# Chaining the four column-group matmuls of each modulation step, with one weight tile per step

## The chip, the core and the metric

The kernel runs on one core of a Trainium2 chip. The metric is device microseconds (us) of one execution, median of three runs. The core has TensorE (PE; its weight loads are shown apart as PEld), VectorE (DVE), ScalarE (ACT), GpSimd (POOL) and SyncE (SP). In this kernel SP issues the transfers from device memory. Each engine takes its instructions in the order of the program, and semaphores tie the engines together.

## The reference, cut to what matters

Two blocks run one after the other on a sequence of 256 tokens, width 1024, all in f32. The first has a hybrid layer (attention with a window, beside a gated delta rule) and a recurrent layer, each followed by an MLP. The second has two layers whose streams (the sequence, and a context of 256 tokens) are scaled and shifted by six vectors of 1024 that come from two conditioning vectors alone:

```python
def modulation(cvec, w_mod, b_mod):
    m = jax.nn.silu(cvec) @ w_mod + b_mod        # w_mod: 1024 x 6144 for each layer
    return jnp.split(m[:, None, :], N_MOD, axis=-1)

    for i in range(DEPTH):                        # second block
        ml = modulation(c, w_mod[i], b_mod[i])
        mc = modulation(c_ctx[None, :], w_mod[i], b_mod[i])
        hl = modulate(rmsnorm(xl, g_pre_mix[i]), ml[0], ml[1])
        ...
```

Nothing in the first block depends on the modulation, so its matmuls can stand anywhere before the second block's layers need them.

## The kernel before, in words

**Main work.** Every large weight matrix is cut into units of 1 MB (tile `wr`, two buffers). ACT rounds each half of a unit to a reduced f32 type (`wh`, line 407), DVE subtracts to get the rest (`wl`, line 408), and PE multiplies `wh` and `wl` with the activations, which are split the same way; results collect in the PSUM tiles `pa`, `pb` and `pc`. Four halves may be held at a time (`NW = 4`). All matmuls go through the helper `mm` (line 342) and all transposes through `tr` (line 366), so that these two lines stand for most of PE's work. Matmuls of the delta rule and of the attention are on plain f32 operands; each f32 matmul leaves two records in the trace.

**Delta rule.** `level` (line 1006 and after) builds a triangular inverse up in six levels for each of two halves of the sequence: POOL makes a masked copy (line 1009), PE multiplies it, ACT copies the product (line 1013), PE multiplies twice more, DVE subtracts (lines 1020 and 1021). After it `delta_out` walks through the two chunks, product by product.

**Modulation.** `mods` (line 749 and after) is a generator of 48 steps: 2 layers x 3 thirds of the 6144 columns x 8 blocks of 128 rows. In one step the two conditioning vectors (`cs_t`, padded to 32 columns) are the stationary operand, and 128 rows x 2048 columns of the weights stream past it as four matmuls of 512 columns. Each of the four writes other 32 partitions of one PSUM bank (`pm`), so each uses another group of 32 columns of the PE array. Eight steps add up into one `pm`; then DVE takes it out (line 782), and some of it goes through device memory (`mdr`).

**Weights of the modulation.** A step's 1 MB comes as two tiles of 512 KB (`wm`, four buffers), loaded by SP in `mod_load` (line 737), two steps ahead. SP's one queue holds these loads and those of `wr` in program order; a load whose buffer is not free holds up what stands behind it.

**Order.** The code calls `fill(n)` at chosen places and weaves the generator between other generators. Then a scheduler orders every engine's instructions by a priority, which is the place in the code unless `tc.high_priority` moves it, and by its own estimate of when an instruction could start. The four matmuls of a step stand in `high_priority(-10)`: ten places later than written.

Of the kernel before, what the change touches and what calls it, by code (L numbers as in the profile page):

```python
# [10 lines left out]
F32 = mybir.dt.float32  # L11
# [4 lines left out]
P = 128  # L16
BIG = 1.0e30
SM = 1.0 / math.sqrt(96.0)
NW = 4
LEAD = 96  # L20
TRAIL = 24
# [9 lines left out]
def _unit(w, k0, nk, cols):  # L31

    n = w.shape[1]
    a = w.reshape(-1, P, n)[k0 : k0 + nk][:, :, cols]
    return a.transpose(1, 0, 2).reshape(P, -1)
# [83 lines left out]
def _ncols(c):  # L119
    return c.stop - c.start if isinstance(c, slice) else len(c)  # L120
# [62 lines left out]
def _consts():  # L183

    parts, at = ([], []), [0, 0]

    def add(name, a, hyb=0):
        a = np.asarray(a, np.float32).reshape(P, -1)
        KC[name] = (hyb, at[hyb], a.shape[1])
        at[hyb] += a.shape[1]  # L190
        parts[hyb].append(a)

    i = np.arange(P)[:, None]
    j = np.arange(P)[None, :]
    add("ident", np.eye(P))
    add("tri", i <= j, 1)
    add("mask_s", np.where(j >= i, BIG, 0.0), 1)
    add("mask_t", np.where(j < i, -BIG, 0.0), 1)
    for s in (1, 2, 4, 8, 16, 32, 64):
        add(f"lv{s}", (i // (2 * s) == j // (2 * s)) & (i % (2 * s) >= s) & (j % (2 * s) < s), 1)  # L200
    add("amask", np.concatenate([np.where(j > i, 0.0, -BIG), np.where(j <= i, 0.0, -BIG)], 1), 1)
    half = 32
    inv = np.float32(10000.0) ** (-np.arange(half, dtype=np.float32) / np.float32(half))
    ang = (np.arange(256, dtype=np.float32)[:, None] * inv[None, :]).astype(np.float32)
    c, s = np.cos(ang.astype(np.float64)), np.sin(ang.astype(np.float64))
    add("cos", np.concatenate([c, c], 1).reshape(2, P, 64).transpose(1, 0, 2), 1)
    add("sin", np.concatenate([-s, s], 1).reshape(2, P, 64).transpose(1, 0, 2), 1)
    inv = (1.0 / (np.float32(10000.0) ** (np.arange(0, 16, 2, dtype=np.float32) / np.float32(16)))).astype(np.float32)
    row = np.repeat(np.arange(4), 64).astype(np.float32)
    col = np.tile(np.arange(64), 4).astype(np.float32)  # L210
    ar, ac = row[:, None] * inv, col[:, None] * inv
    ang = np.concatenate([ar, ar, ac, ac], 1).astype(np.float64)
    c, s = np.cos(ang), np.sin(ang)
    sg = np.where(np.arange(32) % 16 < 8, -1.0, 1.0)
    s = s * sg
    add("acos", c.reshape(2, P, 32).transpose(1, 0, 2))
    add("asin", s.reshape(2, P, 32).transpose(1, 0, 2))
    ft = np.zeros((P, 256))
    ft[64:96] = c.T
    ft[96:128] = s.T  # L220
    ft *= -SM
    add("aft", ft)
    lo = np.arange(P) < 64
    add("one", np.stack([~lo, 0 * lo, lo], 1))
    return [np.ascontiguousarray(np.concatenate(p, axis=1)) for p in parts]


def _pack(inputs):
    def t(name):
        return np.asarray(inputs[name])  # L230

    units = _weight_units(t)
    sizes = [(nk * _ncols(c), nk) for _, _, nk, c in units]
    wp = np.zeros((len(units), P, 2048), np.float32)
    for n, un in enumerate(units):
        a = _unit(*un)
        wp[n, :, : a.shape[1]] = a
    wm = np.ascontiguousarray(
        t("w_mod_2").reshape(2, 8, P, 3, 2, 1024).transpose(0, 3, 1, 4, 2, 5)
    )  # L240
    one = np.ones(1024, np.float32)
    bg = []
    for i in range(2):
        b = t("b_mod_2")[i].reshape(12, 512)
        g = np.concatenate(
            [one, t("g_pre_mix_2")[i], t("g_post_mix_2")[i], one, t("g_pre_mlp_2")[i], t("g_post_mlp_2")[i]]
        ).reshape(12, 512)
        bg.append(np.stack([b, g], 1).reshape(3, 4, 1024))
    cc = np.zeros((P, 8, 32), np.float32)
    cc[:, :, 0] = t("c_2")[0].reshape(8, P).T  # L250
    cc[:, :, 1] = t("c_ctx_2").reshape(8, P).T
    x = t("x")[0]
    kc0, kc1 = _consts()
    arrays = {
        "x": np.ascontiguousarray(x.reshape(2, P, 1024)),
        "xT": np.ascontiguousarray(x.T.reshape(8, P, 256).transpose(1, 0, 2)),
        "ctx": np.ascontiguousarray(t("ctx_2")[0].reshape(2, P, 1024)),
        "wp": wp,
        "wm": wm,
        "bg": np.ascontiguousarray(np.stack(bg)),  # L260
        "cc": cc,
        "cols": np.ascontiguousarray(_cols(t)),
        "rows": _rows(t),
        "kc": kc0,
        "kch": kc1,
    }
    return arrays, sizes
# [26 lines left out]
def hybrid_then_mla(ctx: ExitStack, tc: tile.TileContext, a, out, usizes):  # L294
    nc = tc.nc
    V, S, G, T = nc.vector, nc.scalar, nc.gpsimd, nc.tensor
    cpool = ctx.enter_context(tc.tile_pool(name="cpool", bufs=1))
    wpool = ctx.enter_context(tc.tile_pool(name="wpool", bufs=1))
# [8 lines left out]
    def nm(s):  # L307
        uid[0] += 1
        return f"{s}_{uid[0]}"
# [22 lines left out]
    def psC():  # L332
        return psp.tile([P, 512], F32, tag="pc", bufs=1, name=nm("pc"))

    def psM():
        return psp.tile([P, 512], F32, tag="pm", bufs=1, name=nm("pm"))
# [2 lines left out]
        return ap.bitcast(F32)  # L339

    def mm(o, l, r, start, stop):
        T.matmul(o, l, r, start=start, stop=stop)  # L342

    def v3(ap, n):
        return ap.rearrange("p (a b) -> p a b", a=n)
# [19 lines left out]
    def tr(o, i):  # L365
        T.transpose(o, i, ident)  # L366


    class WS:
        raw, hl, nd, nsp, ng, vec, ahead = {}, {}, 0, 0, 0, set(), 0  # L370
# [24 lines left out]
    def w_split():  # L395
# [5 lines left out]
        r = WS.raw[u][:, o : o + n]  # L401
        h = wpool.tile([P, 1024], F32R, tag="wh", bufs=NW, name=f"wh{i}")
        l = wpool.tile([P, 1024], F32R, tag="wl", bufs=NW, name=f"wl{i}")
        if u in WS.vec:
# [310 lines left out]
    cs_t = cpool.tile([P, 8, 32], F32, name="cs_t")  # L715
# [9 lines left out]
    class WM:  # L725
        tiles, n = {}, 0

    def mod_load():

        if WM.n >= 48:  # L730
            return
        i, q, k = WM.n // 24, WM.n // 8 % 3, WM.n % 8
        for j in range(2):
            wm = wpool.tile([P, 2, 512], F32, tag="wm", bufs=4, name=nm("wm"))
            if WM.n < 2:
                G.tensor_copy(wm[:, 0, 0:1], WM.after)
            nc.sync.dma_start(out=wm, in_=a["wm"][i, q, k, j].rearrange("p (a b) -> p a b", a=2))
            WM.tiles[WM.n, j] = wm
        WM.n += 1

    mc = cpool.tile([P, 2, 3, 32], F32, name="mc")
# [7 lines left out]
    def mods():  # L749

        def cols_of(m, i, q):
            pt = psC()
            for c in range(4):
                tr(pt[:, 128 * c : 128 * c + 128], m[:, 128 * c : 128 * c + 128])
            V.tensor_copy(mc[:, i, q].rearrange("p (c r s) -> p c r s", c=4, r=4),
                          pt.rearrange("p (c r s) -> p c r s", c=4, r=4)[:, :, :, 0:2])

        todo = None
        for n in range(48):
            i, q, k = n // 24, n // 8 % 3, n % 8  # L760
            if k == 0:
                ps = psM()
            if k == 1 and todo:
                cols_of(*todo)
            if k == 4:
                bg = s4([P, 2, 512])
                for r in range(4):
                    nc.sync.dma_start(
                        out=bg[32 * r : 32 * r + 32],
                        in_=a["bg"][i, q, r : r + 1].rearrange("o (a b) -> o a b", a=2).to_broadcast([32, 2, 512]),  # L770
                    )
            while WM.n < min(n + 2, 48):
                mod_load()
            for r in range(4):
                with tc.high_priority(-10):
                    mm(ps[32 * r : 32 * r + 32, :], cs_t[:, k, :], WM.tiles[n, r // 2][:, r % 2, :], k == 0, k == 7)
            mod_load()
            if k < 7:
                yield
                continue  # L780
            m = s2([P, 512])
            V.tensor_tensor(m, ps, bg[:, 0, :], op=ADD)
            V.scalar_tensor_tensor(m, m, K("one")[:, q : q + 1], bg[:, 1, :], op0=ADD, op1=MUL)
            for r in range(4):
                if 2 * q + r // 2 in (2, 5):
                    nc.sync.dma_start(
                        out=mdr[i, :, 2 * q + r // 2, 512 * (r % 2) : 512 * (r % 2) + 512], in_=m[32 * r : 32 * r + 2]
                    )
            todo = (m, i, q)
            yield  # L790
        cols_of(*todo)
        yield
# [796 lines left out]
    def queries(m, s, wq):  # L1589
# [4 lines left out]
        for h2 in range(4):  # L1594
# [7 lines left out]
            if s == 0:  # L1602
                S.activation(qs, p3[0:96], AF.Identity, scale=-SM)
            else:
                S.activation(qs[0:64], p3[0:64], AF.Identity, scale=-SM)
                t1 = s2([P, 2, 256])
# [460 lines left out]
```

## Time and profile before

| | us |
|---|---|
| median of 3 runs | 1634.34 (1633.84 to 1636.41) |
| profiled execution, whole | 1635.88 |
| its span in the trace | 1633.8 |
| PE busy | 1578.0 (97%) |
| DVE busy | 1029.0 (63%) |
| ACT busy | 743.3 (45%) |
| mean granted TensorE clock | 0.991 of full |

Busy time is the time in which at least one instruction of an engine is under way; matmuls overlap in the pipeline, so what a matmul costs is read from start to start of its neighbours, not from its duration. The chain of work that ended last is followed from the last instruction back, at each step to what released it; its shares say on what the end of the program depended.

### The profile page before, as it was taken

To read this page: it belongs to the slowest core of one execution; us is meant where nothing else is said; L and a number is where in the kernel's file an instruction comes from. 1 tells how busy PE (TensorE), PEld (TensorE's weight loads), DVE (VectorE), ACT (ScalarE), POOL (GpSimd) and SP (SyncE) were. 2 spreads that over 40 slices of the span, in tenths; PEclk is the share of its full clock that TensorE was granted. 3 is DMA by queue.
4 is the path that set the end of the run, shared out by engine and by line. 5 is a ranking of instruction groups with operands and counts; after the bars stand their busy time and mean duration, and the time that the engine had idled before them with its cause. 6 is when DMAs were issued, how large, how long until landed. Compare 5 with 4: busy or idle time off the path is not lost.

```text
span 1633.8 us, 24905 instructions
## 1 busy us (share of the span) xinstructions
PE 1578.0 (97%) x10182; PEld 1358.9 (83%) x10182; DVE 1029.0 (63%) x1593; ACT 743.3 (45%) x1264; POOL 94.8 (6%) x121
## 2 busy tenths in 40 slices
PE   7999999999999999999999999999999999989998
PEld 7866679888878998877877789999999788779997
DVE  6874575556787556768974753444444789775555
ACT  5642244443574445436454543222222475554443
POOL 0021000000000000003010100000000030000000
PEclk9999999999999999999999999999999999989999
DMA  7865475555665554562310432222232262235553
GB/s 289 288 217 172 167 258 196 204 207 191 248 258 181 194 192 169 181 227 80 130 52 27 138 134 89 93 103 85 97 104 79 100 216 107 73 126 201 181 186 124
DMA packets 46946, 259.77 MB, mean 159 GB/s; under 512 B 5600, under 2 KB 5856, under 8 KB 24304
## 3 DMA queue, kind: packets, MB, share of 16 engines
q1 hardware_dynamic: 46832, 258.18, 44.9%
q8 instruction: 80, 1.31, 0.3%
q14 instruction: 34, 0.28, 0.1%
HBM read 257.08 MB, written 1.08 MB: 158 GB/s over the span
## 4 chain that ended last, share of the span: by engine, by line
PE 78%; DVE 8%; ACT 4%; DMA 2%; POOL 1%; issue 1%; POOLq 0%; DVEq 0%; ACTq 0%; SPq 0%
PE pa L342 44%; PE pb L342 27%; PE pm L342 4%; PE pb L366 2%; DVE wl L408 1%; DMA wr<-in_wp_dram 1%; PE pc L366 1%; ACT s L1389 1%; ACT wh L407 1%; DVE s L1583 1%; POOL ti L1395 1%; ACT s L1652 0%; DVE s L645 0%; DVE b L711 0%; DVE xt L1426 0%
## 5 line engine op out<-in xcount | busy, mean ns | idle before, releaser
L408 DVE TENSOR_TENSOR wl<-wr,wh 128x1024 fp32r<-128x1024 f32 (+2 forms) x366 | 443.4, 1217 | 301.4 <-ACT wh L407 288.4
L407 ACT CAST wh<-wr 128x1024 fp32r<-128x1024 f32 (+2 forms) x364 | 376.1, 1041 | 405.8 <-PE pa L342 202.6
L342 PE MATMUL pa<-wh,b 128*128 128x512 f32 (+3 forms) x1456 | 411.1, 365 | 12.5 <-ACT b L816 5.7
L342 PE MATMUL pb<-b,wh 128*128 128x256 f32 x2240 | 406.2, 284 | 0.0
L342 PEld LDWEIGHTS pb<-b,wh 128*128 128x128 f32 x2240 | 352.7, 192 | 7.2 <-issue 3.4
L342 PE MATMUL pb<-b,wl 128*128 128x256 f32 x1120 | 317.8, 284 | 0.0
L342 PEld LDWEIGHTS pa<-wh,b 128*128 128x128 f32 x1456 | 267.6, 195 | 57.1 <-ACT b L648 6.1
L342 PE MATMUL pa<-wl,b 128*128 128x512 f32 (+3 forms) x728 | 258.7, 364 | 8.9 <-DVE wl L408 8.9
L342 PE MATMUL pa<-wh,s 128*128 128x512 f32 x768 | 244.5, 391 | 0.0
L342 PEld LDWEIGHTS pb<-b,wl 128*128 128x128 f32 x1120 | 215.1, 192 | 1.7 <-issue 1.7
L342 PE MATMUL pa<-b,wh 128*128 128x256 f32 x1056 | 199.2, 289 | 3.7 <-ACT wh L407 1.9
L342 PEld LDWEIGHTS pa<-b,wh 128*128 128x128 f32 x1056 | 166.2, 193 | 16.0 <-issue 4.4
L342 PEld LDWEIGHTS pa<-wl,b 128*128 128x128 f32 x728 | 142.3, 195 | 35.3 <-DVE wl L408 13.5
L342 PEld LDWEIGHTS pa<-wh,s 128*128 128x128 f32 x768 | 144.4, 188 | 28.9
L342 PE MATMUL pa<-b,wl 128*128 128x256 f32 x528 | 150.1, 288 | 1.3 <-DVE wl L408 1.3
L342 PE MATMUL pa<-wl,s 128*128 128x512 f32 x384 | 150.4, 392 | 0.0
L342 PEld LDWEIGHTS pa<-b,wl 128*128 128x128 f32 x528 | 101.6, 193 | 8.2 <-DVE wl L408 3.3
L560 DVE TENSOR_TENSOR s<-s 128x512 f32<-128x512 f32 x80 | 54.9, 687 | 50.2 <-ACT s L558 50.2
L342 PE MATMUL pm<-wm,cs_t 128*32 128x512 f32 x384 | 83.2, 606 | 1.9 <-DMA wm<-in_wm_dram 1.7
L342 PEld LDWEIGHTS pa<-wl,s 128*128 128x128 f32 x384 | 72.3, 188 | 14.5 <-DVE wl L408 1.2
L1583 DVE SCALAR_TENSOR_TENSOR s<-cu,cols_sb,s 128x512 f32<-128x512 f32 (+1 forms) x120 | 70.7, 621 | 0.5
L366 PE MATMUL pb<-kc_sb,s 128*128 128x128 f32 x366 | 56.8, 279 | 10.8 <-DVE s L1408 2.5
(278 smaller groups left out, 1391.6 us busy)
## 6 DMA issues: line engine op xcount, KB each, us to landing
wr<-in_wp_dram SPq DMA_DIRECT2D x176, 1024.0 KB, 4.8
wm<-in_wm_dram SPq DMA_DIRECT2D x96, 512.0 KB, 5.2
row<-in_rows_dram SPq DMA_DIRECT2D x10, 512.0 KB, 5.5
wr<-in_wp_dram SPq DMA_DIRECT2D x4, 832.0 KB
s<-in_bg_dram SPq DMA_DIRECT2D x24, 128.0 KB, 5.6
row<-mdr SPq DMA_DIRECT2D x6, 512.0 KB, 3.5
wr<-in_wp_dram SPq DMA_DIRECT2D x4, 264.0 KB, 3.6
b<-in_xT_dram SPq DMA_DIRECT2D x4, 256.0 KB, 6.1
```

The costliest lines, as they stand in the source:

```text
L342: T.matmul(o, l, r, start=start, stop=stop)
L366: T.transpose(o, i, ident)
L407: S.copy(h[:, :n], r)
L408: V.tensor_tensor(l[:, :n], r, f(h[:, :n]), op=SUB)
L560: V.tensor_tensor(q, r, r, op=MUL)
L1389: S.activation(j, x, AF.Square, scale=scale, accum_out=o)
L1395: G.tensor_tensor(r, e, half[:, :1], op=POW)
L1583: V.scalar_tensor_tensor(ac, src, w(k), ac, op0=MUL, op1=ADD)
```

## The change

The weights of one step become one tile of 1 MB, and three such tiles are held, loaded three steps ahead; the host packs the array so that a step's rows are contiguous. The four matmuls go through a new helper: the first keeps the priority of before, the last three get a priority ahead of all other work, and each is tied to the one before it by an ordering without a semaphore.

```diff
+AT_ONCE = 100000
-        t("w_mod_2").reshape(2, 8, P, 3, 2, 1024).transpose(0, 3, 1, 4, 2, 5)
+        t("w_mod_2").reshape(2, 8, P, 3, 4, 512).transpose(0, 3, 1, 2, 4, 5)
...
+    def together(mms, ahead=0):
+
+        last = None
+        for m in mms:
+            with tc.high_priority(ahead if last is None else AT_ONCE):
+                i = mm(*m)
+            if last is not None:
+                tc.add_manual_dep(
+                    i.ins, last.ins.name,
+                    mybir.DependencyInfo(mybir.DependencyClass.NoSync, mybir.DependencyReason.DATA),
+                    reason="together",
+                )
+            last = i
...
-        for j in range(2):
-            wm = wpool.tile([P, 2, 512], F32, tag="wm", bufs=4, name=nm("wm"))
-            if WM.n < 2:
-                G.tensor_copy(wm[:, 0, 0:1], WM.after)
-            nc.sync.dma_start(out=wm, in_=a["wm"][i, q, k, j].rearrange("p (a b) -> p a b", a=2))
-            WM.tiles[WM.n, j] = wm
+        wm = wpool.tile([P, 4, 512], F32, tag="wm", bufs=3, name=nm("wm"))
+        if WM.n < 3:
+            G.tensor_copy(wm[:, 0, 0:1], WM.after)
+        nc.sync.dma_start(out=wm, in_=a["wm"][i, q, k])
+        WM.tiles[WM.n] = wm
...
-            while WM.n < min(n + 2, 48):
+            while WM.n < min(n + 3, 48):
                 mod_load()
-            for r in range(4):
-                with tc.high_priority(-10):
-                    mm(ps[32 * r : 32 * r + 32, :], cs_t[:, k, :], WM.tiles[n, r // 2][:, r % 2, :], k == 0, k == 7)
+            together([
+                (ps[32 * r : 32 * r + 32, :], cs_t[:, k, :], WM.tiles[n][:, r, :], k == 0, k == 7) for r in range(4)
+            ], -10)
```

How this moves instructions is seen in the order of the built programs (line 342 of before is line 343 after).

PE at the end of the delta rule's levels, before: `pm` is the modulation's sum, `wm` its weights, `pb` a product of the delta rule.

```order
L342 MATMUL pm_200_1356<-wm_229_1490,cs_t_95 32x512
L342 MATMUL pb_251_1589<-b8_72_767,s2_250_1587 128x128 x4
L342 MATMUL pb_253_1596<-s2_247_1577,b8_66_685 128x128 x2
L342 MATMUL pm_200_1356<-wm_229_1490,cs_t_95 32x512
L342 MATMUL pb_253_1596<-s2_247_1577,b8_66_685 128x128
L342 MATMUL pm_200_1356<-wm_230_1492,cs_t_95 32x512 x2
L342 MATMUL pb_253_1596<-s2_247_1577,b8_66_685 128x128
L342 MATMUL pb_256_1610<-s2_252_1594,b8_66_685 128x128 x4
L342 MATMUL pb_257_1616<-b8_72_767 128x128 x3
L342 MATMUL pm_200_1356<-wm_241_1548,cs_t_95 32x512
```

The same place after:

```order
L343 MATMUL pm_191_1337<-wm_205_1412,cs_t_95 32x512 x4
L343 MATMUL pb_236_1558<-b8_72_767,s2_235_1556 128x128 x4
L343 MATMUL pb_238_1565<-s2_233_1548,b8_66_685 128x128 x4
L343 MATMUL pb_240_1577<-s2_237_1563,b8_66_685 128x128 x4
L343 MATMUL pb_241_1583<-b8_72_767 128x128 x4
L343 MATMUL pm_191_1337<-wm_217_1465,cs_t_95 32x512 x4
L343 MATMUL pb_245_1601<-s2_242_1588,b8_56_527 128x128 x4
```

Before, three single matmuls and a pair of the modulation stand between the pieces of the delta rule's products; after, two whole steps do, and the products between them follow each other.

PE in the MLP of the first layer, before (`b8_290` and `b8_291` are the split activations, `wh84` and `wl84` a half of the weights):

```order
L342 MATMUL pb_403_3406<-b8_290_1743,wl84_3356 128x256
L342 MATMUL pm_273_1673<-wm_359_2736,cs_t_95 32x512
L342 MATMUL pb_403_3406<-b8_290_1743,wh84_3355 128x256
L342 MATMUL pm_273_1673<-wm_359_2736,cs_t_95 32x512
L342 MATMUL pm_273_1673<-wm_360_2738,cs_t_95 32x512 x2
L342 MATMUL pb_403_3406<-b8_291_1744,wh84_3355 128x256
```

After, at one of the three places in this MLP where such a pair of runs stood (at the two others nothing stands now):

```order
L343 MATMUL pb_378_3355<-b8_271_1704,wl84_3307 128x256
L343 MATMUL pb_378_3355<-b8_271_1704,wh84_3306 128x256
L343 MATMUL pm_256_1638<-wm_324_2385,cs_t_95 32x512 x4
L343 MATMUL pb_378_3355<-b8_272_1705,wh84_3306 128x256
L343 MATMUL pb_378_3355<-b8_271_1704,wl84_3307 128x256
```

The step's one and three matmuls have become four in a row.

SP in the delta rule, before:

```order
L737 DMA wm_153_1192<-in_wm_dram 128x1024
L737 DMA wm_154_1194<-in_wm_dram 128x1024
L387 DMA wr13_1753<-in_wp_dram 128x2048
L737 DMA wm_165_1239<-in_wm_dram 128x1024
L737 DMA wm_166_1241<-in_wm_dram 128x1024
L737 DMA wm_175_1281<-in_wm_dram 128x1024
L737 DMA wm_176_1283<-in_wm_dram 128x1024
L387 DMA wr14_1787<-in_wp_dram 128x2048
```

After:

```order
L751 DMA wm_168_1266<-in_wm_dram 128x2048
L751 DMA wm_180_1301<-in_wm_dram 128x2048
L782 DMA s4_227_1512<-in_bg_dram 32x1024 x2
L402 DMA wr13_1714<-in_wp_dram 128x2048
L402 DMA wr14_1748<-in_wp_dram 128x2048
L2042 DMA xc0_4662<-in_ctx_dram 128x1024
L2042 DMA xc1_4664<-in_ctx_dram 128x1024
L751 DMA wm_192_1342<-in_wm_dram 128x2048
```

One load of 1 MB stands where two of 512 KB stood, and `wr14` stands ahead of the step after, no longer behind it.

## Rows read from the trace of the kernel before

**Rows 1.** Page: span, engine shares of the chain, the modulation's matmuls, loads.

```profile
span 1633.8 us, 24905 instructions
...
PE 78%; DVE 8%; ACT 4%; DMA 2%; POOL 1%; issue 1%; POOLq 0%; DVEq 0%; ACTq 0%; SPq 0%
...
L342 PE MATMUL pm<-wm,cs_t 128*32 128x512 f32 x384 | 83.2, 606 | 1.9 <-DMA wm<-in_wm_dram 1.7
...
wr<-in_wp_dram SPq DMA_DIRECT2D x176, 1024.0 KB, 4.8
```

**Rows 2.** Chain by line: 90:187, 187:222, 222:400, 400:417, 417:480, 760:790, 1330:1352 us.

```profile
by line: PE pb L342 44.0%; PE pm L342 28.8%; PE pa L342 10.8%; PE pb L366 4.2%; PE pa L366 2.5%; ACT s L963 2.1%; DVE s L996 1.7%; PE pc L366 1.1%; POOL rq L461 1.0%; POOL ti L461 1.0%; issue 1.0%; DVE s L1061 0.7%; DVE s L1062 0.7%; DVE b 
...
by line: PE pa L342 72.3%; PE pm L342 20.0%; PE pb L366 5.7%; PE pc L366 2.5%
...
by line: PE pa L342 50.6%; PE pb L342 45.9%; PE pm L342 3.3%; PE pb L366 0.2%
...
by line: PE pa L342 57.1%; PE pm L342 28.0%; PE pc L366 8.6%; PE pb L366 7.8%
...
by line: DMA wr<-in_wp_dram 26.0%; DVE wl L408 16.8%; DVE b L711 9.5%; DVE b L1365 7.5%; ACT wh L407 6.7%; issue 5.8%; DVE b L1363 3.9%; ACT b L1360 3.2%; DVE b L1269 2.9%; DVE b L1357 2.8%; ACT L1360 2.0%; DVE s L1319 2.0%; ACT b L1268 1.8
...
by line: PE pa L342 51.3%; PE pm L342 9.4%; DVE b L1608 7.0%; DVE s L1607 6.9%; ACT b L1498 6.4%; ACT b L1621 3.9%; ACT b L1620 3.9%; ACT s L1627 3.6%; PE pb L366 3.4%; issue 1.8%; ACT b L1605 1.6%; ACT b L1496 1.2%
...
by line: PE pa L342 74.5%; PE pm L342 22.5%; PE pb L366 4.0%
```

**Rows 3.** Chain in order of time, delta rule: start us, us, what (records).

```profile
98.50 0.98 PE pm L342 x2
99.47 3.09 PE pb L342 x24
102.57 0.99 PE pm L342 x8
...
134.46 1.09 PE pb L342 x8
135.55 0.98 PE pm L342 x2
...
136.94 0.98 PE pm L342 x4
...
141.62 1.83 PE pm L342 x10
```

**Rows 4.** Timeline, 102:104 us: start, us, engine, line, operation, idle before.

```profile
102.50 1.06 PE L342 MATMUL pm<-wm,cs_t 128*32 128x512 f32 x8
102.66 0.58 ACT L1013 COPY s<-pb 128x512 f32<-128x512 f32 x1 [0.69 <-PE pb L342]
...
103.49 0.71 PE L342 MATMUL pb<-s,b 128*128 128x128 f32 x4
```

**Rows 5.** Instructions on tile wm: what PE waited for; transfers.

```profile
DMA wm<-in_wm_dram: 5.3, 5
...
DMA to landing us min/median/max: 3.4/5.2/8.4
```

**Rows 6.** Chain in order of time, 690:706 us.

```profile
694.76 0.98 PE pm L342 x2
...
698.15 1.05 PE pm L342 x7
...
699.54 4.22 DMA wm<-in_wm_dram
...
703.80 1.05 PE pm L342 x4
```

**Rows 7.** Stretches: us, busy (count) of PE, PEld, DVE, ACT, POOL, clock, DMA, GB/s.

```profile
90.00:187.00 97.00, 95.30 (x621) 60.54 (x621) 48.61 (x96) 29.84 (x96) 17.09 (x14) 1.00 0.59 208
480.00:490.00 10.00, 8.28 (x29) 6.69 (x30) 8.42 (x11) 2.48 (x4) 0.00 (x0) 0.83 0.86 327
...
40.00:50.00 10.00, 10.00 (x87) 10.00 (x86) 7.45 (x13) 8.37 (x28) 0.00 (x0) 1.00 0.91 334
```

More of the change, by code (lines that the diff above doesn't have):

```diff
@@ L341, in mm @@
     def mm(o, l, r, start, stop):
-        T.matmul(o, l, r, start=start, stop=stop)
+        return T.matmul(o, l, r, start=start, stop=stop)
+    def together(mms, ahead=0):
[10 more added lines that the diff above has]
+            last = i
     def v3(ap, n):
```

## The prediction

> **What bounds the kernel now.** I read the page first: the chain that ended last is PE for 78% of the span, DVE for 8%, ACT for 4% [rows 1]. So time on PE is worth its length almost everywhere, and the question is how long the modulation holds PE and where. The page's group of its matmuls gives 606 ns each for 384 records [rows 1]; times the count that is 233 us, but its busy time, overlaps merged, is 83.2 us [rows 1]. The records overlap, so neither duration prices a matmul.
>
> The chain in order of time does. A run of modulation matmuls between other work holds PE for 0.98 us when it has two records, which is one matmul, for 0.98 us with four and for 0.99 us with eight, which is four matmuls [rows 3]. Four matmuls on four different column groups go side by side and cost as much as one. A fifth on a group that is already taken starts again: ten records take 1.83 us, 0.84 more [rows 3]. What counts is therefore the number of runs, not of matmuls. Each run also delays its start: 24 records of the delta rule ahead of one take 3.09 us, eight take 1.09 [rows 3], so sixteen more cost 2.00, eight are worth 1.00, and 0.09 us goes to the entry.
>
> Next, the chain by line, stretch by stretch: the modulation's share times the length of the stretch is its time on the chain [rows 2]. It is 28.8% of 97 us = 27.9 in the delta rule and attention (90 to 187 us), 20.0% of 35 = 7.0 in 187 to 222, 3.3% of 178 = 5.9 in the GEMMs of 222 to 400, 28.0% of 17 = 4.8 in 400 to 417, 9.4% of 30 = 2.8 in 760 to 790 and 22.5% of 22 = 4.95 in 1330 to 1352. In 417 to 480 it does not appear: there the chain goes through the loads of `wr` (26.0%) and DVE (16.8% for `wl` alone) [rows 2], and PE saved there is worth nothing.
>
> **The change, part by part.** *The chained matmuls.* In the built order the 192 matmuls stand in 70 runs before, many of one or three, and in 40 after: 34 of four, four of eight, two of twelve. By place, with 0.99 us for a run and 0.84 for each further four:
>
> - 90 to 187: 15 runs are left, 15.0 instead of 27.9, saves 12.9.
> - 187 to 222: five, 5.0 instead of 7.0, saves 2.0.
> - 222 to 400: one step, 1.0 instead of 5.9, saves 4.9.
> - 400 to 417: one of eight and two of four, 3.8 instead of 4.8, saves 1.0.
> - 760 to 790: none; those steps now stand near 750 us, where the chain does not pass through them. Saves 2.8.
> - 1330 to 1352: two, 2.0 instead of 4.95, saves 2.95.
>
> That is 26.6 us. On these stretches about 53 runs become 26; 27 entries at 0.09 are 2.4 more.
>
> *One place with a load on the chain.* At 699.54 us the chain waits 4.22 us for a tile that could be loaded only when a run that began at 698.15 had read its buffer [rows 6]. In the new order the buffer belongs to the step that begins at 694.76 and is read whole by 695.7. With 4.8 us for a load of 1 MB, as `wr` takes [rows 1], it lands at 700.5 and the matmuls after it start there instead of at 703.80 [rows 6]. That is 3.3 us at best; a step that moved in front costs up to 0.84 of it and other loads may share the engines, so I take 2.0.
>
> Gross: 26.6 + 2.4 + 2.0 = 31.0 us.
>
> *What comes back: the runs were also cover.* In a level of the delta rule PE finishes a product, ACT copies it, PE goes on with the copy. Before, a run filled the hop: it starts at 102.50, ACT's copy begins at 102.66, lasts 0.58 and ends at 103.24, PE goes on at 103.49 [rows 4]. Without the run PE would wait 0.74 us, so there only a quarter of a microsecond is saved. In the new order most such hops still have a step or a product of the other half between them: four of the first levels keep one run each. I find the hop nearly bare at three places (the last product of the second level, the last level, the product after `delta_out`'s start). Further waits arise where `pm` must be taken out by DVE between the eighth step and the next with few products between. All thirteen removed runs as bare hops would be 13 x 0.74 = 9.6 us, none would be 0; I take 3.5, as the order shows cover for more than half.
>
> *The loads.* Bytes stay the same, transfers halve in number. In the first 50 us a third tile is asked for: 1 MB more ahead of `wr8`, and 512 KB that stood there moves behind. At the 334 GB/s of 40 to 50 us, with the DMA engines 91% busy [rows 7], 1 MB takes 3.1 us, so the delay lies between 0 and 3.1; I take 1.5, the net 512 KB. Later, SP's queue keeps the pace of before, since each step's tile is freed as a whole and `wr14` is even asked for before the step that it followed. The wait for modulation weights was 5.3 us in five places [rows 5], and three tiles hold one step more than four half tiles. I put that at 0; it could gain the 3 us not counted above or lose about as much, if the four last steps of the delta rule, which stand some 4 us from the freeing of their tile to its next use, wait the rest of 4.8 us each.
>
> *The next bound.* PE arrives earlier at places where ACT and DVE also work at the chain's edge: 760 to 790 has DVE and ACT groups of 7.0%, 6.9% and 6.4% on it [rows 2]. For that I take 2.0 of the 5.75 saved there and in 1330 to 1352; bounds 0 and 5.75.
>
> Sum: 31.0 - 3.5 - 1.5 - 2.0 = 24.0 us. The profiled execution has a span of 1633.8 and took 1635.88 in all, 1.5 above the median of 1634.34; it would become 1611.9, the median 1610.3. I say 1610.
>
> **The rivals.** *The cover was all that the cut-in runs were.* Then the delta stretch saves nothing: 12.9 and its 13 entries (1.2) go, with the 3.5 that are then no longer to be paid back. 31.0 - 14.1 - 1.5 - 2.0 = 13.4, so 1621. For it: PE's work between a product and its copy is under 1 us in a level [rows 4]. Against it: two independent halves and the attention are woven there, DVE is busy for 48.61 and ACT for 29.84 of 97 us [rows 7], so neither is short of time.
>
> *Loads that land too late: slower.* The place is the delta stretch: 15 steps in some 84 us, each PE queue held by the first matmul of a step until 1 MB has landed, and the delta rule's products stand behind it. If loads went one at a time, they would eat the whole gain of 24 us from (84 + 24) / 15 = 7.2 us each. Half a tile has taken up to 8.4 us and 5.2 in the median [rows 5]; two such one after the other, 10.4, would make the stretch 156 us and the kernel 1682. Against it: a load of the same 1 MB takes 4.8 [rows 1], the halves were asked for in pairs and shared the engines, the stretch moves 208 GB/s against 334 earlier [rows 7], and with three tiles loads overlap.
>
> *The clock.* In 480 to 490 us PE was busy for 8.28 of 10 us, and the granted clock was 0.83 in the mean: a third of that time at 1.2 GHz instead of 2.4, 1.7 us of PE's work. In 90 to 187 us it is 1.00, with PE busy for 95.30 of 97 [rows 7]. If bare hops brought such a fall once for each of the 15 runs left, 25 us would be lost and the time would be 1635, no change; more than that, slower. The Trainium skill's page "TensorE: Matmul & The Clock Gate" (Part 1, and "HAM oscillation") says that the slow clock is the default, that activity releases it and that idle gaps between bursts bring it back; by that rule taking filler from PE can cost what it saves. The trace agrees that falls follow waits, but the waits that I expect in the delta rule are 0.74 us and alone, so I count none.
>
> *No effect.* The order has no run left that is not four, eight or twelve, and rows 3 show four at the price of one, so this remains only for a group that would not overlap for another reason.
>
> **How the numbers follow.** Forecast 0.76, cover 0.15, late loads 0.04, clock 0.03, no effect 0.02. The forecast's own range is 1603 (nothing comes back) to 1619 (most hops bare, early load at its bound, half of the edge lost). With the cover rival and some room for small unseen waits the range of 8 in 10 is 1602 to 1625. A measurement of this kernel can tell 0.2%, 3.3 us, from no change: faster means under 1631.1. The first two cases are faster but for 0.01; the clock and no effect share 0.04 for the same; late loads and the tails give 0.06 for slower.
>
> **What would show it.** Right: the modulation's busy time on PE falls from 83.2 to about 47 us, its matmuls start within hundredths of a microsecond of each other in fours, and its share of the chain falls from 28.8% to about 18% in the delta stretch, which ends some 10 us earlier. The GEMMs of 222 to 400 lose 4.9 us with no new wait. The cover step is wrong if PE's waits for ACT's copies in the levels sum to much more than 3.5 us; the load step, if PE waits for `wm` much over 5.3 us or for `wr` in the first 60 us over 1.5 us more. The whole is wrong if runs of four take clearly longer than 0.99 us, or if the stretches without modulation (480 to 690, 950 to 1290 us) change their length.

## The result, and the profile after

The changed kernel takes **1610.58 us** (median of 4 runs, 1607.37 to 1612.86) against 1635.38 for the kernel before (1633.84 to 1637.1) in the same session: 0.9847 of it, 95% interval 0.9826 to 0.9867. That is 24.8 us less; the forecast was 24.0 less and 1610. The total was right; of its terms the mechanism held, and four sizes did not.

The page of the profiled execution (1610.15 us whole), to be read against [rows 1]:

```profile
span 1608.1 us, 24812 instructions
...
PE 79%; DVE 11%; ACT 5%; POOL 2%; issue 2%; DMA 1%; SPq 0%; POOLq 0%; DVEq 0%; ACTq 0%
...
wm<-in_wm_dram SPq DMA_DIRECT2D x48, 1024.0 KB, 6.3
```

The groups of PE by line, the modulation's matmuls (count | busy us, mean ns | idle before):

```profile
L343 PE MATMUL pm<-wm,cs_t 128*32 128x512 f32 x384 | 49.7, 603 | 0.1
```

Busy time falls from the 83.2 us of [rows 1] to 49.7 (about 47 was forecast), while one record lasts as long as before: more of them overlap. The chain in order of time in the delta rule (start us, us, what), answering to [rows 3]:

```profile
90.79 0.99 PE pm L343 x8
91.79 1.09 PE pb L343 x8
92.88 0.99 PE pm L343 x8
93.87 3.09 PE pb L343 x24
96.96 0.99 PE pm L343 x8
```

Every run shown is a whole step of eight records for 0.99 us; runs of two and four records are gone. Next, stretches of both kernels between the same pair of matmuls with `wh` or `wl` (of which both have 8280 records). Columns as in [rows 7]: start and end, length, busy us of PE, PEld, DVE, ACT and POOL with counts, granted clock, DMA share, GB/s. Before:

```profile
86.90:239.40 152.50, 150.12 (x939) 103.49 (x938) 90.57 (x166) 50.77 (x125) 20.66 (x17) 1.00 0.58 205
239.40:424.00 184.60, 184.60 (x1153) 159.46 (x1152) 105.16 (x114) 80.57 (x94) 1.84 (x2) 1.00 0.59 208
714.20:794.30 80.10, 76.37 (x522) 65.95 (x521) 63.32 (x113) 43.80 (x97) 13.26 (x20) 0.98 0.39 140
1313.60:1430.50 116.90, 111.37 (x770) 93.13 (x769) 99.15 (x203) 69.19 (x144) 18.00 (x28) 1.00 0.35 122
```

After:

```profile
85.50:222.60 137.10, 133.84 (x948) 101.31 (x947) 89.85 (x166) 50.59 (x125) 21.88 (x17) 1.00 0.64 241
222.60:400.10 177.50, 177.50 (x1154) 158.23 (x1153) 104.95 (x114) 80.52 (x94) 1.84 (x2) 1.00 0.60 210
690.10:770.10 80.00, 72.54 (x513) 64.81 (x512) 63.19 (x113) 43.71 (x97) 12.91 (x20) 1.00 0.37 138
1290.10:1407.20 117.10, 109.19 (x756) 92.32 (x755) 99.38 (x204) 69.17 (x144) 18.53 (x28) 1.00 0.30 104
```

In the first two rows the stretch is shorter by what PE is less busy: 15.4 and 7.1 us. In the last two PE is less busy by 3.8 and 2.2 us and the stretch is as long as before: there the time became idle time of PE. All of the span, by such marks:

| place (us, after) | forecast gain | measured gain |
|---|---|---|
| up to 85.5 | -1.5 | 1.4 |
| 85.5 to 222.6, delta rule and output | 12.9 + 2.0 + 1.35 - 3.5 = 12.75 | 15.4 |
| 222.6 to 400.1, GEMMs | 4.9 + 1.0 + 0.5 = 6.4 | 7.1 |
| 400 to 530 | 0 | -1.7 |
| 600 to 690, the load | 2.0 | 1.9 |
| 690 to 830 and 1290 to 1407 | 2.8 + 2.95 + 0.45 - 2.0 = 4.2 | -0.7 - 0.2 = -0.9 |
| 1407 to 1430 (before: 1430 to 1456) | 0 | 2.4 |
| all of it, with 0.1 elsewhere | 24 | 25.7 |

### The profile page after: what moved, and what is told of

The parts are those of the page before. It is cut to its first block, busy times and chain, and to the rows that moved or that the text cites. A ratio compares the mean times of both kernels' runs of the same rounds, so it can differ in the third digit from the quotient of the medians.

```text
span 1608.1 us, 24812 instructions
## 1 busy us (share of the span) xinstructions
PE 1544.7 (96%) x10182; PEld 1351.4 (84%) x10182; DVE 1028.5 (64%) x1593; ACT 742.7 (46%) x1264; POOL 96.7 (6%) x120
## 4 chain that ended last, share of the span: by engine, by line
PE 79%; DVE 11%; ACT 5%; POOL 2%; issue 2%; DMA 1%; SPq 0%; POOLq 0%; DVEq 0%; ACTq 0%
PE pa L343 46%; PE pb L343 27%; DVE wl L423 2%; PE pb L381 2%; PE pm L343 2%; DVE s L1597 1%; PE pc L381 1%; ACT s L1403 1%; ACT wh L422 1%; POOL ti L1409 1%; ACT s L1666 1%; DMA wr<-in_wp_dram 0%; DMA wm<-in_wm_dram 0%; POOL ti L476 0%; DVE s L660 0%
## 5 line engine op out<-in xcount | busy, mean ns | idle before, releaser
L1409 POOL TENSOR_TENSOR ti<-ti,half 128x1 f32<-128x1 f32 x26 | 22.2, 853 | 763.5 <-DVE ti L1408 763.5
```

The source lines that it names most:

```text
L1409: G.tensor_tensor(r, e, half[:, :1], op=POW)
```

## The experiments

Theory: a run of modulation matmuls holds PE for its own length (0.99 us for up to four on four column groups) plus an entry, nearly all of it on the chain; so time goes with the number of runs. Rivals: the runs are only cover for hops; the gain comes from the larger tile and the third buffer; the overlap depends on the order of the matmuls.

| kernel | runs | median us | ratio to before, 95% |
|---|---|---|---|
| before | 70 | 1635.4 | 1 |
| tile alone | 63 | 1629.1 | 0.9961 (0.9944 to 0.9977) |
| chain alone | 49 | 1616.2 | 0.9880 (0.9864 to 0.9897) |
| two tiles held | 43 | 1609.7 | 0.9847 (0.9830 to 0.9863) |
| changed | 40 | 1610.6 | 0.9847 (0.9826 to 0.9867) |
| steps in pairs | 33 | 1611.4 | 0.9864 (0.9841 to 0.9888) |

**The two parts alone.** First the chain without the new tile (two half tiles a step, as before):

```diff
-        wm = wpool.tile([P, 4, 512], F32, tag="wm", bufs=3, name=nm("wm"))
...
+        for j in range(2):
+            wm = wpool.tile([P, 2, 512], F32, tag="wm", bufs=4, name=nm("wm"))
```

> The change without its tile part: chained matmuls, but a step's weights still come as two tiles of 512 KB, four held, loaded two steps ahead. In its order the 192 matmuls stand in 49 runs (31 of four, 12 of two, 4 of eight) against 70 before and 40 after. Theory of the runs (each run holds PE for 1.0 us and costs 0.1 to 0.2 us to enter, a further four in it 0.84): 21 fewer runs, three quarters of them on the chain, about 18 us less than before, so 1612 to 1620. Rival, the load side (one larger load for two, one step more held) makes the gain: no change, 1632 to 1638.

Then the tile without the chain:

```diff
-            together([
-                (ps[32 * r : 32 * r + 32, :], cs_t[:, k, :], WM.tiles[n][:, r, :], k == 0, k == 7) for r in range(4)
-            ], -10)
+            for r in range(4):
+                with tc.high_priority(-10):
+                    mm(ps[32 * r : 32 * r + 32, :], cs_t[:, k, :], WM.tiles[n][:, r, :], k == 0, k == 7)
```

> The tile part alone: one tile of 1 MB for a step, three held, but the four matmuls unchained at their old priority. In its order they stand in 63 runs, 21 of one matmul. Theory of the runs: seven fewer runs, three quarters on the chain, 4 to 8 us less than before, 1626 to 1632. Rival, the load side: nearly the whole gain, 1608 to 1615.

1616.22 and 1629.14 us, both as expected (of the 49 runs, two more are of six). The chain carries most of the gain. By the theory of the runs, the tile helps because matmuls that wait for one tile fall together (63 runs for 70), and because a chained step is not cut in half by its second load (40 runs for 49).

**Two tiles held instead of three.**

```diff
-        wm = wpool.tile([P, 4, 512], F32, tag="wm", bufs=3, name=nm("wm"))
+        wm = wpool.tile([P, 4, 512], F32, tag="wm", bufs=2, name=nm("wm"))
...
-            while WM.n < min(n + 3, 48):
+            while WM.n < min(n + 2, 48):
```

> The changed kernel with two tiles of weights held instead of three, each asked for one step later; 43 runs instead of 40. If loads overlap steps well enough with two tiles (a load lands after 4.7 to 8.6 us, and the steps of the delta rule stand about 6.8 us apart), only the three runs more count, 3 us: 1612 to 1615 us. If the third tile is what covers the loads, each of the some 15 steps of the delta rule waits up to 2 us for its tile: 1625 to 1645 us.

1609.7 us (1609.2 to 1610.61), the changed kernel's time and below both ranges; the three further runs cost nothing that can be measured. What waits for the tile `wm` in this kernel (us, times; min/median/max):

```profile
DMA wm<-in_wm_dram: 1.2, 2
...
DMA to landing us min/median/max: 4.7/5.9/9.4
```

PE waits 1.2 us for these weights in the whole program, against 5.3 in [rows 5] and 1.0 in the changed kernel. The third buffer is worth nothing; down to 43 runs each removed run brought (1634.7 - 1609.7) / 27 = 0.93 us (1634.7 is the kernel before in the same session), and then no more.

**Each step's matmuls twice, in two orders.** The extra matmuls change the sums. In the order 0 1 2 3 0 1 2 3:

```diff
-                ... WM.tiles[n][:, r, :], k == 0, k == 7) for r in range(4)
+                ... WM.tiles[n][:, r, :], k == 0 and not d, k == 7 and d) for d in (False, True) for r in range(4)
```

> After, but each step's four matmuls are issued twice, in the order of groups 0 1 2 3 0 1 2 3 (the modulation's sums come out doubled). Theory: the second four cost 0.84 us a step on PE, 40 us over 48 steps, and some 33 of the steps stand on the chain: 28 to 40 us more than after, 1638 to 1650. Rival, the time of the modulation on PE is hidden under the other engines and its gain came from order: under 8 us more, 1610 to 1618.

In the order 0 0 1 1 2 2 3 3 (`for r in range(4) for d in (False, True)`):

> As the kernel with each step's matmuls issued twice, but in the order 0 0 1 1 2 2 3 3, so that each matmul is followed by one on its own column group (the modulation's sums come out doubled). Theory that a matmul waits for the one before it on the same columns and runs beside one on others: five slots a step instead of two, 0.99 + 4 x 0.84 = 4.35 us instead of 1.83, 121 us more over 48 steps than with the order 0 1 2 3 0 1 2 3, most of it on the chain: 1720 to 1770. Rival, matmuls of 32 columns overlap whatever their group: the same as in the other order, 1638 to 1650.

1635.62 and 1633.2 us (one execution each). The first is 2 us below its range; the second expectation was wrong by 87 us and more. The chain in order of time, one run of each; the first order:

```profile
106.01 1.85 PE pm L343 x16
```

And the second:

```profile
104.79 1.87 PE pm L343 x16
```

The order inside a run does not matter. Had the second matmul on a group held up what stands behind it, 0 0 1 1 2 2 3 3 would cost several times 0.84 more. The start times in the traces say the same: in either order the sixteen records of a run begin in four waves of four, 0.43 to 0.45 us apart.

**All four matmuls of a step on one column group** (in the 36 steps with k from 1 to 6; the sums are then not those of the reference).

```diff
-                (ps[32 * r : 32 * r + 32, :], ...) for r in range(4)
+                (ps[32 * g : 32 * g + 32, :], ...) for r in range(4) for g in [r if k in (0, 7) else 0]
```

> In the changed kernel all four matmuls of a step go to the first group of columns (36 of the 48 steps), so their sums land in one place and are wrong. If the overlap comes from the groups' own columns, a step costs four times 0.86 instead of one run of 0.99, about 2.55 us more on PE, 92 us over 36 steps, of which some 60% stand on the chain as with the doubled steps: 1650 to 1690 us. If four matmuls overlap whatever columns they use, the time stays at about 1611 us.

1670.91 us (one execution), inside the first range. The chain in order of time:

```profile
97.32 3.55 PE pm L343 x8
```

The same eight records take 3.55 us on one group and 0.99 on four; on one group they begin one by one, 0.43 to 0.45 us apart. Together: a matmul waits for those ahead of it on its own columns, and matmuls of other groups behind it go past; a run lasts as long as its fullest group. So the program's order, in which an engine takes its instructions, binds these matmuls only within a group. (In the one-group kernel the four also add into the same place of `pm`; no run parts the columns from the place.) Of 36 x 2.56 = 92 us more on PE, 60.3 reached the end; of 41 us of doubled matmuls, 25.

**Steps of the delta rule left out.** Eleven of its steps issue no matmuls, first in the changed kernel, then in the kernel before (their sums are missing).

```diff
+SKIP = (3, 4, 5, 6, 9, 10, 11, 12, 13, 14, 17)
...
+            if n not in SKIP:
```

> The modulation matmuls of eleven steps in the delta rule (n 3 to 6, 9 to 14 and 17) are left out of the changed kernel, so their sums are not computed: 30 runs of these matmuls stay of 40. If a run costs what it holds PE and covers little, eleven runs by about 1.14 us, less some four bare hops of 0.74, are gone: about 1600 us (1598 to 1603). If every run that stays in the delta rule covers a hop of 0.74 us, only 11 x 0.4 = 4.4 us go: about 1606 us.

> The same matmuls are left out of the kernel before: 51 runs stay of 70. If a run costs what it holds PE, 19 runs by 0.9 to 1.1 us are gone: 1615 to 1619 us. If the runs cover hops of 0.74 us that stay bare without them, 19 x (1.1 - 0.74) = 7 us go: about 1628 us.

1606.01 and 1619.51 us (one execution each). The first whole time missed its range and looks like the rival's, so the delta rule itself has to be read. Before, changed, changed with steps left out, before with steps left out, each in its own fence:

```profile
86.90:202.30 115.40, 113.02 (x698) 74.59 (x697) 62.16 (x113) 34.09 (x102) 19.66 (x16) 1.00 0.55 193
```

```profile
85.50:187.70 102.20, 99.06 (x691) 72.84 (x690) 61.46 (x113) 33.90 (x101) 20.89 (x16) 1.00 0.59 219
```

```profile
84.80:178.30 93.50, 87.55 (x604) 70.67 (x603) 62.56 (x113) 33.84 (x101) 20.59 (x16) 1.00 0.60 215
```

```profile
84.10:182.00 97.90, 91.72 (x610) 71.25 (x609) 64.42 (x113) 34.01 (x101) 22.68 (x16) 1.00 0.62 214
```

Length less PE's busy time is PE's idle time: 2.38, 3.14, 5.95 and 6.18 us. The change took 13 runs out of here for 0.76 us of new idle time. Eleven more steps (ten runs) cost 2.81 (0.28 a run) and bring 8.70 of the 11.51 that PE is less busy; taking 19 runs from the kernel before costs 3.80 and brings 17.5 of 21.3. The cover rival would have had 4.4 and 7. So cover exists, and grows as runs become rare, but it is at most a quarter of a run's price. In the whole profiled execution only 4.1 of the 8.70 us are left: 0.7 were gained ahead of the delta rule, and 5.3 lost behind it, 2.2 of them to the clock at 1400 to 1426 us (below), 2.1 between 400 and 530 and 1.1 between 690 and 830 us.

**Four steps moved into a wait.** Four steps leave the delta rule for the stretch of the recurrent layer's output product, where PE waits for DVE. While `ORD.hold` is set, each step is also tied behind the last matmul that stands ahead of them all (the lines in the helper are left out here).

```diff
-            for _ in range(18):
+            for _ in range(14):
...
-        fill(2)
+        ORD.hold = True
+        fill(6)
+        ORD.hold = False
```

> Four steps of the changed kernel move from the delta rule to the wait behind the recurrent layer's output product, where PE stands idle for several us (468 to 492 us) while VectorE normalises. If a run costs what it holds PE and the idle time covers it, four runs of about 1 us leave the chain: 2 to 5 us below the changed kernel, 1605 to 1609 us. If the runs lengthen that wait, or if they covered hops where they stood, there is no gain: 1611 us or above.

1619.32 us (ratio to before 0.9904, 0.9885 to 0.9923): worse than the changed kernel. The delta rule did lose 4.7 us, 1.17 per run. But more than four steps moved: in the changed kernel eight stand between 379 and 422 us and none from there to 672; here two stand at 375 and nine between 478 and 503 us. And 500 to 530 us (on the changed kernel's scale) became 5.6 longer. SP's queue in this kernel (start us, from first start to last end, line, transfer, count):

```profile
487.00 5.71 SPq L757 DMA_DIRECT2D wm<-in_wm_dram  x3
492.76 0.43 SPq L469 DMA_DIRECT2D row<-in_rows_dram  x1
493.24 1.06 SPq L408 DMA_DIRECT2D wr<-in_wp_dram  x2
```

And its PE (in brackets the idle time before):

```profile
499.67 2.78 PE L346 MATMUL pm<-wm,cs_t 128*32 128x512 f32 x24
504.36 0.50 PE L346 MATMUL pb<-b,wh 128*128 128x256 f32 x2 [1.91 <-ACT wh L428]
```

The moved steps brought their loads along. The main weights `wr`, asked for in the changed kernel from 485.2 us on, stand behind `wm` here and go out at 493.24; PE then waits 1.91 us for them. Ahead of that wait, behind the last output product, stand three of the steps (2.78), at a place where PE does not wait at all in the changed kernel. A further 2.1 us went at 461 to 500 us, and 2.2 at 400 to 417, where the steps are gone and this kernel's PE waits. What each of these delays costs alone was not tried.

**Steps in pairs.** Every second step issues eight matmuls in one chain; the load asked for behind each step is now asked for behind every second one.

```diff
+            if k % 2:
+                together([
+                    (ps[32 * r : 32 * r + 32, :], cs_t[:, j, :], WM.tiles[n - k + j][:, r, :], j == 0, j == 7)
+                    for j in (k - 1, k) for r in range(4)
+                ], -10)
```

> Every second step of the changed kernel issues its own four matmuls and those of the step before, eight in one chain: 33 runs instead of 40, the same matmuls. A run of eight holds PE 1.85 us and two runs of four hold it 2 x 0.99 with an entry each of 0.1 to 0.2, so seven runs fewer give 7 x 0.3 = 2 us: 1606 to 1610 us. If two steps at once wait for their weights, or leave bare the hops between which they stood, the time is that of the changed kernel or above: 1611 us or more.

1611.45 us (1610.07 to 1618.57): no gain, as the rival had it. The loads are not the reason: PE waits 1.4 us for these weights, 1.0 in the changed kernel. PE's modulation runs sum up to 46.6 us instead of 49.2, so the 2.6 us were saved on PE; but the delta rule and its output became 1.4 us longer, and the clock took 2.0 at the end. No version beats the changed kernel.

## Why the prediction was right, and where it was not

**Four for the price of one: right.** The mechanism that carried the forecast holds: 0.99 us a run, and with 15 runs fewer between 85.5 and 222.6 us PE is 150.12 - 133.84 = 16.28 us less busy, 1.085 each, which is the predicted 0.99 + 0.09. That it comes from the columns, as I had it, the one-group kernel shows; that the order does not matter I had not expected. On the Trainium skill's page "TensorE: Matmul & The Clock Gate" (Part 3) matmuls start and end strictly in program order. That does not agree with 1.87 us for the order 0 0 1 1 2 2 3 3; the records don't name their column group, so this is shown by the time and by the waves of starts.

**The entry: too small in the GEMMs.** From 222.6 to 400.1 us ten runs became four. The runs themselves fell by 10.66 - 4.84 = 5.8 us, the stretch, in which PE is never idle, by 7.1: 1.3 / 6 = 0.22 us an entry instead of 0.09. The page "TensorEngine Tiling (Array Packing)" of the Trainium skill (Key Properties) says that a change of tiling mode drains the engine; it gives no figure, and the trace has 0.09 beside the delta rule's small products and 0.22 beside wide ones.

**The cover: too dear.** The step "13 x 0.74 = 9.6, I take 3.5" failed in size: the delta rule and its output have 3.26 us of idle PE after 2.38 before, so 0.9 came back. The share of the modulation in the chain from 90 to 176 us fell to 12.6% instead of 18%, since near 110 to 124 us the chain now goes through DVE and POOL.

**The early load: not there.** I took 1.5 us for the third tile in front of `wr8`. The mark at 86.9 us before is reached at 84.2 by the kernel with that tile and no chain, and at 84.1 by the one that has the kernel before's loads. That the kernel before was 2.7 us slower than both is not the load: 1.3 us of it are its clock. Stretch 18 to 22 us before, then with its steps left out (the same program up to there):

```profile
18.00:22.00 4.00, 3.91 (x20) 3.91 (x21) 3.96 (x10) 2.67 (x6) 1.55 (x4) 0.57 0.83 286
```

```profile
18.00:22.00 4.00, 4.00 (x36) 4.00 (x35) 3.83 (x14) 1.46 (x3) 0.36 (x3) 1.00 0.91 325
```

At 0.57 most of it ran at 1.2 GHz: 20 matmuls where the other has 36. The other 1.4 us were lost ahead of 18.8 us, where the kernel before has a clock of 0.99 and PE waits longer; what for was not followed. The chain itself cost something that I had not counted: the same work, from 40 to 85.5 us of the changed kernel, takes it 45.5 us, with the chain alone 45.5, before 44.8.

**The load at 699 us: right in size, not in kind.** 1.9 us for 2.0. But the chain still waits for a modulation tile there, only while PE has other work:

```profile
686.11 7.76 DMA wm<-in_wm_dram
...
693.91 1.07 PE pm L343 x8
```

It lands at 693.86 in the middle of a run of three steps that takes 3.03 instead of 2.71 us, so the wait costs 0.3.

**The next bound: the step that failed.** I took 2.0 of 5.75 us for it at 760 and 1330 us; it took all of the gain and 0.9 more. [Rows 2] had DVE and ACT on 7.0, 6.9 and 6.4% of the first stretch; in the second PE alone stood on the chain, and I read that as room. In the first, the chain in order of time before has

```profile
778.22 1.84 PE pm L342 x12
```

between two pieces of PE's work on `pa`. At the same place in the changed kernel PE is idle for 2.06 us, and the chain goes through DVE and ACT:

```profile
751.87 2.21 DVE wl L423
...
755.23 0.57 ACT s L1666 x2
...
755.84 3.13 PE pa L343 x24
```

The run had filled a hop. The changed kernel's chain in the second:

```profile
1324.34 1.72 DVE wl L423
...
1326.07 0.70 DVE b L1622
...
1326.79 0.69 DVE s L1621
...
1328.22 1.23 DVE wl L423
1329.45 3.01 DVE s L1597 x5
...
1333.21 0.79 ACT s L1666 x2
...
1334.04 2.05 PE pa L343 x15
```

The runs that went had covered DVE, which is busy for 99 of 117 us there in either kernel, and splits `wl` for weights ahead of the sums that PE waits for. The kernel with every step doubled settles it: its three steps there hold PE for 5.56 us, the changed kernel's two for 1.99, and the same stretch is shorter than in either kernel:

```profile
1318.00:1432.60 114.60, 111.35 (x788) 93.25 (x787) 98.92 (x202) 68.00 (x141) 17.00 (x27) 1.00 0.33 110
```

The kernel with steps in pairs has no step there at all and takes 114.9 us. So the modulation on PE doesn't set its length. In the first stretch it does once the hops are full: the doubled steps make that one 6.2 us longer. DVE's order in the second differs from kernel to kernel, by the place of a `wl` before or after two or three sums; whether this order alone makes 114.6 or 117.1 us of the stretch was not tried.

**The clock: it moved time at the ends, not in the delta rule.** The granted clock is 1.00 all through 85.5 to 222.6 us, so that rival is out. It fell elsewhere, behind waits. In the changed kernel:

```profile
453.00:461.00 8.00, 4.79 (x12) 3.58 (x13) 8.00 (x11) 0.97 (x2) 0.00 (x0) 0.57 0.26 77
484.00:492.00 8.00, 6.77 (x32) 6.53 (x32) 6.21 (x10) 0.41 (x1) 0.99 (x1) 0.57 0.68 217
1407.00:1418.00 11.00, 6.85 (x37) 5.80 (x36) 9.48 (x20) 8.28 (x16) 1.22 (x3) 0.93 0.36 134
1418.00:1430.00 12.00, 9.98 (x74) 9.38 (x74) 8.87 (x18) 4.55 (x12) 1.40 (x1) 0.92 0.25 87
```

In the kernel before:

```profile
482.00:487.00 5.00, 5.00 (x16) 3.92 (x16) 4.92 (x7) 1.23 (x2) 0.00 (x0) 0.66 0.98 350
509.00:515.00 6.00, 5.76 (x36) 5.53 (x36) 5.27 (x8) 1.07 (x2) 0.99 (x1) 0.72 0.84 274
1430.00:1442.00 12.00, 7.86 (x39) 6.78 (x38) 10.48 (x21) 8.56 (x17) 1.51 (x3) 0.85 0.36 132
1442.00:1456.00 14.00, 11.99 (x74) 11.51 (x74) 8.16 (x17) 4.55 (x12) 1.40 (x1) 0.76 0.21 75
```

Of the 1.7 us lost between 400 and 530 us a wait is the larger part. PE comes to the weights of 450 us 24.5 us earlier than before, but DVE has split them only 22.0 us earlier:

```profile
456.21 0.79 PE L343 MATMUL pa<-wl,b 128*128 128x512 f32 x1 [5.67 <-DVE wl L423]
```

Before, fourteen records of the modulation filled 1.92 us of this wait, and PE was idle for 1.28. That costs 2.5 us. Behind it both kernels run at 1.2 GHz for a while (the first row of each), the changed one for less: 1.6 come back. In the second rows it is the other way, and 1.3 go to the clock; the rest of the stretch gains 0.5.

The 2.4 us gained at 1407 to 1430 are the clock's and not the change's: with the delta rule's steps left out, the kernel has the changed one's program there and the clock of the kernel before. In that kernel:

```profile
1400.00:1412.00 12.00, 7.86 (x40) 6.70 (x39) 10.45 (x22) 8.27 (x17) 1.64 (x3) 0.85 0.46 172
1412.00:1426.00 14.00, 11.99 (x74) 11.51 (x74) 8.55 (x18) 4.63 (x12) 1.40 (x1) 0.76 0.22 76
```

Over the profiles of all twelve kernels this piece takes either 22.8 to 23.1 or 24.8 to 25.3 us, and either value occurs with the chain and without.

So the near agreement, 24.0 and 25.7, is partly luck: cover, entry, the slow start of the kernel before and the clock at the end gave 8.6 us more than forecast (2.65 + 0.7 + 2.9 + 2.4), the next bound and 400 to 530 us 6.8 less. What holds is the middle: 22.5 us from fewer runs between 85.5 and 400 us, where 19.2 were forecast.

## What to carry to other kernels

Price small matmuls by the start of the next other instruction, in runs: put those of different column groups next to each other, and don't mind their order. Before counting a saved run as time, look at every engine's busy share in its stretch: where DVE is busy for 79 to 85% of it, all of PE's saved time turned into idle time here. When filler work is moved into a wait, its loads move too, and in one queue they can stand ahead of what ends the wait, as they did here.

## What had not been expected of the hardware

- The column groups each keep their own order: 16 records in the order 0 0 1 1 2 2 3 3 take 1.87 us, in 0 1 2 3 0 1 2 3 1.85, and eight records on one group 3.55.
- Entering and leaving a 32-column run costs 0.09 us beside 128-column products of the delta rule and 0.22 us beside the wide products of the GEMMs.
- The same instructions run at 1.2 GHz for different times in different executions: at the end of the program the granted clock is 0.92 to 0.93 in one profile and 0.76 to 0.85 in another, which alone moves the end by 2.2 us.
